# Seven of eleven gate/up chunks by seven products, with weight sums made by accumulating loads

## The chip, the cores and the metric

One core of one Trainium2 chip runs the whole layer as one program. Engines: PE (TensorE, matmuls into PSUM), PEld (its weight loads), DVE (VectorE), ACT (ScalarE), POOL (GpSimd), SP (issues DMAs). The metric is the device time of one execution in microseconds; the median of three runs of the kernel before is 2265.83 us (2264.74 to 2266.03).

## The reference

A layer of 256 tokens, width 2048, float32: a feed-forward, a mixer (mLSTM and stick-breaking attention), a second feed-forward, each followed by a layer norm, then a gated embedding. What the change touches is the feed-forward, of width 5632, run twice:

```
h = silu(x @ w1) * (x @ w3)        # gate and up, 2048 -> 5632
y = h @ w2                         # down, 5632 -> 2048
x = layer_norm(alpha * x + 0.5 * y)
```

## The kernel before

**Precision and weights.** Every product is made of three matmuls: activations and weights are split into a high and a low part (fp32r), and high·high, high·low and low·high are summed in PSUM (lines 990 to 992). A weight tile is 256 rows by 512 columns, 512 KB. It goes through `loads` (SP issues the DMA into a `raw` tile), then `split_one`: ACT casts the high half (L943), DVE subtracts for the low half (L945). `limits` says how many raw tiles and how many split weights may be held at once: in the feed-forwards 8 raws and 7 splits. One split weight takes two of the 44 pages of 4 KB per partition, a raw one.

**Units.** A `Unit` is one weight tile against one half of the tokens (128 rows): 2 row blocks x 3 matmuls = 6 matmuls of 128x512. `program` is the list of all units in the order in which PE runs them; side work (evictions, transposes) is scheduled between them by due times in `DELAY`. After each unit `splits_due` issues splits ahead, as far as `limits` allows, and each freed raw lets `loads` issue the next DMA. PE, DVE, ACT, POOL and SP each run their own instructions in that order.

**Direct chunks.** The width 5632 is cut into 11 chunks of 512 columns. `up(c)` does a chunk directly: 16 weight tiles (8 of w1, 8 of w3), each used by both token halves, 32 units. Gate results get SiLU on ACT, then DVE multiplies them with the up results (L388) and `turn` transposes the hidden tile on PE (L234); ACT and DVE split the transposed tile (L228, L229) into `hT`. `down(c, m)` multiplies m chunks of hidden by w2: 16 units per chunk, 8 weight tiles per chunk, and one DVE addition into `xres` per 512 columns, token half and call (L435).

**Seven-product chunks.** `up7(c)` does a chunk by a scheme of seven block products in place of eight (Winograd's form of Strassen's). The two token halves are the rows, the two halves of a 512-row group of the inner dimension the middle, and w1 and w3 the two column blocks. It takes 28 units with 28 weights: 8 raw weights for products 1 and 2, and for each of four row groups i five: products 5, 7, 6, 4, 3. The weights of the last five are b11, b12 (w1 and w3, first half of the group), b21, b22 (second half) and their sums, made by DVE in place (L295) by `minus`:

```
T1 = b12 - b11   (product 5)      T3 = b22 - b12   (product 7)
T2 = b22 - T1    (product 6)      T4 = b21 - T2    (product 4)      b22 (product 3)
```

Each row group takes four loads and four such subtractions. The matching sums of the activations ("forms") are made once per 512 columns by `form_turn` (L254). At the end of a product `done` combines the results in PSUM on DVE (L397).

**Order.** `weave(main, side)` spreads the units of one seven-product chunk evenly through a list of direct units. Before, each feed-forward has five woven stretches, one for each of chunks 1, 3, 5, 7 and 9; the other six chunks are direct. In the middle of it a stretch is gate(c), down of two earlier chunks, up(c), 64 units, with the 28 of the seven-product chunk between.

Of the kernel before, what the change touches and what calls it, by code (L numbers as in the profile page):

```python
# [11 lines left out]
ALU = mybir.AluOpType  # L12
# [14 lines left out]
TEMP_BUFS = 6  # L27


RAW_FFN, RAW_MIX, RAW_EDGE = 8, 5, 4  # L30
SPLIT_FFN, SPLIT_MIX, SPLIT_EDGE = 7, 6, 11
EDGE = 6
PSUM_BUFS = 8
SKEW = 6
# [12 lines left out]
class Sched:  # L47


    def __init__(self):  # L50
        self.now = 0.0
        self.heap = []
        self.count = 0
# [46 lines left out]
class Raw:  # L100


    def __init__(self, src, cols):
        self.src, self.cols, self.tile = src, cols, None


class Weight:
# [38 lines left out]
def flat(pairs):  # L146
    return [u for p in pairs for u in p]


def skewed(pairs):  # L150
    return [p[0] for p in pairs] + [p[1] for p in pairs]
# [3 lines left out]
def kernel(  # L155
# [6 lines left out]
    nc = tc.nc  # L162
    x, out = x[0], out[0]
# [56 lines left out]
    def load_x(c, t):  # L220
        cs = slice(c * COL, (c + 1) * COL)
        nc.sync.dma_start(out=xres[t][:, cs], in_=x[t * P:(t + 1) * P, cs])
# [22 lines left out]
    def form_turn(act, c):  # L245

        a = [act.whole[c][:, t * COL:(t + 1) * COL] for t in range(TT)]
        s12, s34 = temp(), temp()
        l, r = slice(0, 2 * P), slice(2 * P, 4 * P)
        for dst, in0, in1, op in ((s12[:, l], a[1][:, l], a[1][:, r], ALU.add),  # L250
                                  (s12[:, r], s12[:, l], a[0][:, l], ALU.subtract),
                                  (s34[:, l], a[0][:, l], a[1][:, l], ALU.subtract),
                                  (s34[:, r], a[0][:, r], s12[:, r], ALU.subtract)):
            nc.vector.tensor_tensor(out=dst, in0=in0, in1=in1, op=op)  # L254
        for h, src in enumerate((s12, s34)):
            dst = act.forms.get(c, h)
            split_psum(dst[:, 0], dst[:, 1], src.rearrange("q (k s) -> q k s", s=P))
            drop()
            act.forms.mark(c, h, 4)
        return  # L260
        yield
# [19 lines left out]
    def seven(wa, wb, rows, col0, cols, act, done):  # L281

        n = rows // (4 * P)
        accs = {m: {} for m in range(1, 8)}

        def unit(m, i, tile, src, half, sub):  # L290
            return Unit(tile, half, accs[m], src, i, sub, i == 0, i == n - 1, lambda ps, t, m=m: done(m, ps))

        def minus(out, a, b):
            def make():
                nc.vector.tensor_tensor(out=out.tile[:, :, :cols], in0=a.tile[:, :, :cols], in1=b.tile[:, :, :cols],  # L295
                                        op=ALU.subtract)
            return make

        units = []
        for m, sub in ((1, 0), (2, 2)):  # L300
            for i in range(n):
                units.append(unit(m, i, plain(rows_of(wa, (4 * i + sub) * P, col0, cols)), act, 0, sub))
        for i in range(n):
            b11, b12, b22, b21 = (rows_of(w, (4 * i + sub) * P, col0, cols)
                                  for w, sub in ((wa, 0), (wb, 0), (wb, 2), (wa, 2)))
            units += [
                unit(5, i, Weight(b11, [b11, b12], [], minus(b11, b12, b11)), act.forms, 0, 0),
                unit(7, i, Weight(b12, [b22], [b12], minus(b12, b22, b12)), act.forms, 1, 0),
                unit(6, i, Weight(b11, [], [], minus(b11, b22, b11)), act.forms, 0, 2),
                unit(4, i, Weight(b21, [b21], [b11, b21], minus(b21, b11, b21)), act, 1, 2),  # L310
                unit(3, i, Weight(b22, [], [b22]), act.forms, 1, 2),
            ]
        return units

    program = []
# [54 lines left out]
    def ffn(w1, w3, w2, act, norm, skew=True):  # L370
        n = FF // COL
        hT = ActT(act_tile)

        def turn(src, c, t):
            transposed(src, hT, c, t)
            drop()
            return
            yield

        def up(c):  # L380
            s = {}

            def gate(ps, t):
                s[t] = temp()
                activate(s[t][:], ps, ACT.Silu)

            def hidden(ps, t):
                nc.vector.tensor_tensor(out=s[t][:], in0=ps, in1=s[t][:], op=ALU.mult)  # L388
                sched.spawn(turn(s[t], c, t), DELAY["h"] + 2.0 * t)

            return group(w1, 0, D, c * COL, COL, act, gate), group(w3, 0, D, c * COL, COL, act, hidden)

        def up7(c):
            r, held = {}, {}

            def both(out, a, b, op):
                nc.vector.tensor_tensor(out=out, in0=a, in1=b, op=op)  # L397

            def done(m, ps):
                held[m] = ps  # L400
                if m == 1:
                    r["u"] = temp()
                    nc.scalar.copy(r["u"][:], ps)
                elif m == 2:
                    r["g0"] = temp()
                    both(r["g0"][:], ps, r["u"][:], ALU.add)
                    activate(r["g0"][:], r["g0"][:], ACT.Silu)
                elif m == 6:
                    u, v, z = r["u"], temp(), temp()
                    both(u[:], ps, u[:], ALU.add)  # L410
                    both(v[:], held[5], u[:], ALU.add)
                    both(u[:], held[7], u[:], ALU.add)
                    both(z[:], held[5], u[:], ALU.add)
                    r["v"], r["z"] = v, z
                elif m == 4:
                    u, z = r["u"], r["z"]
                    both(u[:], u[:], ps, ALU.subtract)
                    activate(u[:], u[:], ACT.Silu)
                elif m == 3:
                    u, v, z = r["u"], r["v"], r["z"]  # L420
                    both(v[:], ps, v[:], ALU.add)
                    both(v[:], v[:], r["g0"][:], ALU.mult)
                    both(z[:], z[:], u[:], ALU.mult)
                    drop(2)
                    sched.spawn(turn(v, c, 0), DELAY["h"])
                    sched.spawn(turn(z, c, 1), DELAY["h"] + 2.0)

            return seven(w1, w3, D, c * COL, COL, act, done)

        def down(c, m):  # L430
            pairs = []
            for g in range(D // COL):
                def add(ps, t, g=g):
                    xs = xres[t][:, g * COL:(g + 1) * COL]
                    nc.vector.scalar_tensor_tensor(out=xs, in0=ps, scalar=0.5, in1=xs,  # L435
                                                   op0=ALU.mult, op1=ALU.add)
                    if c + m == n:
                        norm.chunk(t, g)
                pairs += group(w2, c * COL, m * COL, g * COL, COL, hT, add, c)
            return pairs  # L440

        gate, hidden = up(0)
        program.extend((skewed(gate[:SKEW]) if skew else flat(gate[:SKEW])) + flat(gate[SKEW:]))
        gate2, hidden2 = up(2)
        program.extend(weave(flat(hidden + gate2 + down(0, 1) + hidden2), up7(1)))
        for c in range(4, n - 1, 2):
            gate, hidden = up(c)
            program.extend(weave(flat(gate + down(c - 3, 2) + hidden), up7(c - 1)))
        gate, hidden = up(n - 1)
        mid = down(n - 4, 2)  # L450
        program.extend(weave(flat(gate + hidden + mid[:12]), up7(n - 2)))
        program.append(norm.load)
        program.extend(flat(mid[12:] + down(n - 2, 1)))
        tail = down(n - 1, 1)
        program.extend(flat(tail[:-SKEW]) + skewed(tail[-SKEW:]))
        boundary(True)
# [457 lines left out]
    def loads(most=len(raws)):  # L914
        while pos["load"] < most and pos["raw"] < limits(pos["split"])[0]:
            j = pos["load"]
            r = raws[j]
            r.tile = page_pool.tile([P, 2, COL], F32, name="raw", tag="page")
            for ks in pieces(j):
                nc.sync.dma_start(out=r.tile[:, ks, :r.cols], in_=r.src[:, ks])  # L920
                if j == 0 and ks.start == 0:
                    load_x(0, 1)
            pos["load"] += 1
            pos["raw"] += 1

# [24 lines left out]
        loads()  # L950

    def splits_due():
        most = pos["at"] + 3 if pos["at"] < 5 else len(weights)
        while pos["split"] < most and len(splits) < limits(pos["split"])[1]:
            split_one()

# [71 lines left out]
```

## Time and profile before

| | |
|---|---|
| Median of 3 runs | 2265.83 us |
| Profiled execution: time, span | 2265.87 us, 2264.1 us |
| Granted clock of PE, mean | 0.996 |
| Busy: PE, DVE, ACT, POOL | 2235.6, 1652.4, 1137.3, 45.6 us |
| Bytes moved, mean rate | 476.65 MB, 211 GB/s |
| Queue of SP's DMAs, share of the 16 engines' span | 66.9% |
| Weight splits on DVE (L945) | 941, 1106.9 us |
| Weight sums on DVE (L295) | 160, 195.0 us |

How to read it: busy time is a sum over stages that differ, so the stages are looked at one by one. In a line of a group the numbers after the bar are its busy time, the mean of one in ns, and the idle time of its engine just before it with what ended it. A line of waits has who waited for whom: total us, times, longest. A line of a stretch has, for each engine, busy us and instructions, then the granted clock, the share of the DMA engines and GB/s.

### The profile page before, as it was taken

The numbers are of one execution on the slowest core, as the hardware profiler recorded it, in microseconds if no ns is written. First come the engines' busy times: TensorE is split into PE (matmuls) and PEld (weight loads), VectorE is DVE, ScalarE is ACT, GpSimd is POOL, SyncE is SP. The second block draws the span as 40 slices with busy tenths as digits, with TensorE's granted clock in tenths as the row PEclk, the third lists the DMA queues.
The fourth block names the chain that finished last, engine by engine and source line by source line (L and its number), as shares of the span: only waits on it lengthen the run. The fifth ranks groups of instructions, "written<-read, shape, count | busy, mean of one in ns | idle before, by whom it ended". The sixth has DMA issues, their size and how long they took to land.

```text
span 2264.1 us, 27326 instructions
## 1 busy us (share of the span) xinstructions
PE 2235.6 (99%) x10203; PEld 1851.5 (82%) x10203; DVE 1652.4 (73%) x1806; ACT 1137.3 (50%) x1327; POOL 45.6 (2%) x47
## 2 busy tenths in 40 slices
PE   8999999999999999999999999999999999999999
PEld 6888888888887888888888888778888888888878
DVE  5888878788888765654445466698787878887873
ACT  6545555555552555544643354355545545464452
POOL 2000000000000000100100000200000000000000
PEclk9999999999999999999999999999999999999999
DMA  8676767767783665565566676567677777777543
GB/s 303 217 240 217 248 209 247 234 215 242 251 277 110 206 187 160 169 185 158 167 183 189 186 227 213 174 205 243 204 243 229 223 241 233 241 237 260 196 152 100
DMA packets 249798, 476.65 MB, mean 211 GB/s; under 512 B 14976, under 2 KB 24000, under 8 KB 249664
## 3 DMA queue, kind: packets, MB, share of 16 engines
q1 hardware_dynamic: 249664, 474.90, 66.9%
q8 instruction: 80, 1.31, 0.2%
q14 instruction: 54, 0.44, 0.1%
HBM read 472.74 MB, written 2.10 MB: 210 GB/s over the span
## 4 chain that ended last, share of the span: by engine, by line
PE 93%; DVE 4%; DMA 1%; ACT 1%; issue 1%; SPq 0%; ACTq 0%; DVEq 0%
PE mm L992 30%; PE mm L990 30%; PE mm L991 30%; DMA raw<-in_ffn_w_dram 1%; PE ms L234 1%; DVE split L945 1%; DVE xres L352 1%; DVE xres L353 0%; ACT split L943 0%; DVE xres L350 0%; DVE actT L229 0%; DVE stats L337 0%; PE ms L715 0%; PE ms L738 0%; PE ms L666 0%
## 5 line engine op out<-in xcount | busy, mean ns | idle before, releaser
L945 DVE TENSOR_TENSOR split<-raw,split 128x1024 fp32r<-128x1024 f32 (+1 forms) x941 | 1106.9, 1203 | 343.0 <-ACT split L943 332.2
L990 PE MATMUL mm<-split,actT 128*128 128x512 f32 (+2 forms) x3200 | 1246.8, 390 | 4.8 <-ACT actT L228 4.8
L992 PE MATMUL mm<-split,actT 128*128 128x512 f32 (+2 forms) x3200 | 1236.9, 387 | 10.1 <-DVE actT L229 10.1
L991 PE MATMUL mm<-split,actT 128*128 128x512 f32 (+2 forms) x3200 | 1235.2, 386 | 0.7 <-DVE split L945 0.6
L943 ACT CAST split<-raw 128x1024 fp32r<-128x1024 f32 (+1 forms) x941 | 937.8, 1036 | 500.6 <-DVE raw L295 185.3
L992 PEld LDWEIGHTS mm<-split,actT 128*128 128x128 f32 x3200 | 602.8, 188 | 135.3 <-DVE actT L229 13.8
L990 PEld LDWEIGHTS mm<-split,actT 128*128 128x128 f32 x3200 | 603.3, 189 | 123.6 <-ACT actT L228 6.3
L991 PEld LDWEIGHTS mm<-split,actT 128*128 128x128 f32 x3200 | 603.3, 189 | 119.4 <-DVE split L945 1.9
L295 DVE TENSOR_TENSOR raw<-raw 128x1024 f32<-128x1024 f32 x160 | 195.0, 1219 | 0.0
L228 ACT CAST actT<-ms 128x512 fp32r<-128x512 f32 (+2 forms) x110 | 55.6, 522 | 133.2 <-PE ms L234 104.8
L435 DVE SCALAR_TENSOR_TENSOR xres<-mm,xres 128x512 f32<-128x512 f32 x112 | 76.9, 689 | 49.6 <-PE mm L992 49.4
L229 DVE TENSOR_TENSOR actT<-ms,actT 128x512 fp32r<-128x512 f32 (+2 forms) x110 | 64.2, 603 | 32.0 <-ACT actT L228 32.0
L206 ACT ACTIVATE temp<-temp 128x512 f32<-128x512 f32 (+1 forms) x36 | 21.0, 585 | 115.9 <-DVE temp L397 93.7
L397 DVE TENSOR_TENSOR temp<-mm,temp 128x512 f32<-128x512 f32 x60 | 41.4, 690 | 36.5 <-PE mm L992 35.5
L206 ACT ACTIVATE temp<-mm 128x512 f32<-128x512 f32 (+1 forms) x34 | 19.2, 572 | 64.5 <-PE mm L992 64.4
L206 ACT ACTIVATE big<-mm 128x512 f32<-128x512 f32 x20 | 12.0, 598 | 55.8 <-PE mm L992 55.8
L786 DVE TENSOR_TENSOR big<-mm,big 128x512 f32<-128x512 f32 x16 | 11.1, 692 | 30.0 <-PE mm L992 30.0
L872 DVE TENSOR_TENSOR temp<-temp,big 128x512 f32<-128x512 f32 (+1 forms) x10 | 5.8, 584 | 37.0 <-ACT temp L206 37.0
L367 POOL TENSOR_SCALAR xres<-xres 128x512 f32<-128x512 f32 x16 | 25.7, 1607 | 333.4 <-DVE xres L350 300.5
L202 ACT ACT_TABLE_LOAD x25 | 32.1, 1283 | 0.4
L206 ACT ACTIVATE rstd<-mv,eps 128x1 f32<-128x1 f32 x6 | 1.8, 295 | 53.9 <-DVE mv L343 53.9
L614 DVE SCALAR_TENSOR_TENSOR temp<-ms,cw,temp 128x253 f32<-128x253 f32 (+2 forms) x48 | 23.1, 481 | 7.4 <-ACT temp L206 6.2
(109 smaller groups left out, 473.7 us busy)
## 6 DMA issues: line engine op xcount, KB each, us to landing
raw<-in_ffn_w_dram SPq DMA_DIRECT2D x607, 512.0 KB, 4.7
raw<-in_w_in_dram SPq DMA_DIRECT2D x168, 512.0 KB, 3.8
raw<-in_w_out_dram SPq DMA_DIRECT2D x32, 512.0 KB, 5.0
raw<-in_w_ple_gate_dram SPq DMA_DIRECT2D x24, 512.0 KB, 4.7
raw<-in_w_up_m_dram SPq DMA_DIRECT2D x16, 512.0 KB, 3.7
raw<-in_w_up_sb_dram SPq DMA_DIRECT2D x16, 512.0 KB, 4.8
raw<-in_w_ple_gate_dram SPq DMA_DIRECT2D x16, 256.0 KB, 5.0
big<-in_ln_g_dram SPq DMA_DIRECT2D x6, 512.0 KB, 6.6
```

The costliest lines, as they stand in the source:

```text
L202: nc.scalar.preload_act_table_set(table[0])
L206: nc.scalar.activation(out, in_, func, **kw)
L228: nc.scalar.copy(hi, ps)
L229: nc.vector.tensor_tensor(out=lo, in0=ps, in1=hi, op=ALU.subtract)
L295: nc.vector.tensor_tensor(out=out.tile[:, :, :cols], in0=a.tile[:, :, :cols], in1=b.tile[:, :, :cols], op=ALU.subtract)
L397: nc.vector.tensor_tensor(out=out, in0=a, in1=b, op=op)
L435: nc.vector.scalar_tensor_tensor(out=xs, in0=ps, scalar=0.5, in1=xs, op0=ALU.mult, op1=ALU.add)
L943: nc.scalar.copy(hi[:, ks], r[:, ks])
L945: nc.vector.tensor_tensor(out=lo[:, ks], in0=r[:, ks], in1=hi[:, ks], op=ALU.subtract)
L990: nc.tensor.matmul(ps, hi, w[0][:, k, :u.cols], start=first, stop=False)
L991: nc.tensor.matmul(ps, hi, w[1][:, k, :u.cols], start=False, stop=False)
L992: nc.tensor.matmul(ps, lo, w[0][:, k, :u.cols], start=False, stop=last)
```

## The change

Seven chunks of each feed-forward (1, 2, 4, 5, 7, 8, 10) are done by seven products, four (0, 3, 6, 9) directly. All seven are woven as one list of 196 units into one list of 248 direct units; gate 0 and eight units of up 0 go ahead, and the rest of the down product follows.

The weight sums change sign: T1 = b12 + b11, T3 = b12 + b22, T2 = T1 + b22, T4 = b21 + T2, and the forms and the PSUM work take the signs up (`scalar=-1.0` in two places). T1 is no longer made by DVE: b12 is loaded by SP into the tile, and POOL issues a second load of b11 that adds into it (`accum_op`). T3 is made so for odd i, from a load of its own of b12; for even i it is a load of b12 to which DVE adds b22. T2 and T4 stay DVE's. In the feed-forwards nine raws and six split weights are held, and the limit of the first splits (`splits_due`) holds until weight 7 instead of 5.

```diff
-RAW_FFN, RAW_MIX, RAW_EDGE = 8, 5, 4
-SPLIT_FFN, SPLIT_MIX, SPLIT_EDGE = 7, 6, 11
+RAW_FFN, RAW_MIX, RAW_EDGE = 9, 5, 4
+SPLIT_FFN, SPLIT_MIX, SPLIT_EDGE = 6, 6, 11
...
-        for dst, in0, in1, op in ((s12[:, l], a[1][:, l], a[1][:, r], ALU.add),
-                                  (s12[:, r], s12[:, l], a[0][:, l], ALU.subtract),
-                                  (s34[:, l], a[0][:, l], a[1][:, l], ALU.subtract),
-                                  (s34[:, r], a[0][:, r], s12[:, r], ALU.subtract)):
-            nc.vector.tensor_tensor(out=dst, in0=in0, in1=in1, op=op)
+        nc.vector.tensor_tensor(out=s12[:, l], in0=a[1][:, r], in1=a[1][:, l], op=ALU.subtract)
+        nc.vector.scalar_tensor_tensor(out=s12[:, r], in0=s12[:, l], scalar=-1.0, in1=a[0][:, l],
+                                       op0=ALU.mult, op1=ALU.subtract)
+        nc.vector.tensor_tensor(out=s34[:, l], in0=a[0][:, l], in1=a[1][:, l], op=ALU.subtract)
+        nc.vector.tensor_tensor(out=s34[:, r], in0=a[0][:, r], in1=s12[:, r], op=ALU.add)
...
-        def minus(out, a, b):
+        def plus(out, a, b):
             def make():
                 nc.vector.tensor_tensor(out=out.tile[:, :, :cols], in0=a.tile[:, :, :cols], in1=b.tile[:, :, :cols],
-                                        op=ALU.subtract)
+                                        op=ALU.add)
...
+            t1 = Raw(b12.src, cols, b11.src)
+            t3, add = (Raw(b12.src, cols, b22.src), None) if i % 2 else (b12, plus(b12, b12, b22))
             units += [
-                unit(5, i, Weight(b11, [b11, b12], [], minus(b11, b12, b11)), act.forms, 0, 0),
-                unit(7, i, Weight(b12, [b22], [b12], minus(b12, b22, b12)), act.forms, 1, 0),
-                unit(6, i, Weight(b11, [], [], minus(b11, b22, b11)), act.forms, 0, 2),
-                unit(4, i, Weight(b21, [b21], [b11, b21], minus(b21, b11, b21)), act, 1, 2),
+                unit(5, i, Weight(t1, [t1], []), act.forms, 0, 0),
+                unit(7, i, Weight(t3, [t3, b22], [t3], add), act.forms, 1, 0),
+                unit(6, i, Weight(t1, [], [], plus(t1, t1, b22)), act.forms, 0, 2),
+                unit(4, i, Weight(b21, [b21], [t1, b21], plus(b21, t1, b21)), act, 1, 2),
                 unit(3, i, Weight(b22, [], [b22]), act.forms, 1, 2),
             ]
...
-        gate, hidden = up(0)
-        program.extend((skewed(gate[:SKEW]) if skew else flat(gate[:SKEW])) + flat(gate[SKEW:]))
-        gate2, hidden2 = up(2)
-        program.extend(weave(flat(hidden + gate2 + down(0, 1) + hidden2), up7(1)))
-        for c in range(4, n - 1, 2):
-            gate, hidden = up(c)
-            program.extend(weave(flat(gate + down(c - 3, 2) + hidden), up7(c - 1)))
-        gate, hidden = up(n - 1)
-        mid = down(n - 4, 2)
-        program.extend(weave(flat(gate + hidden + mid[:12]), up7(n - 2)))
+        gate, hidden = zip(*(up(c) for c in (0, 3, 6, 9)))
+        program.extend((skewed(gate[0][:SKEW]) if skew else flat(gate[0][:SKEW])) + flat(gate[0][SKEW:]))
+        last = down(8, 2)
+        main = flat(hidden[0] + down(0, 1) + gate[1] + down(1, 1) + hidden[1] + down(2, 2)
+                    + gate[2] + down(4, 1) + hidden[2] + down(5, 2)
+                    + gate[3] + down(7, 1) + hidden[3] + last[:8])
+        program.extend(main[:8] + weave(main[8:], [u for c in (1, 2, 4, 5, 7, 8, 10) for u in up7(c)]))
         program.append(norm.load)
-        program.extend(flat(mid[12:] + down(n - 2, 1)))
+        program.extend(flat(last[8:]))
...
+            if r.plus is not None:
+                nc.gpsimd.dma_start(out=r.tile[:, :, :r.cols], in_=r.plus, accum_op=ALU.add)
...
-        most = pos["at"] + 3 if pos["at"] < 5 else len(weights)
+        most = pos["at"] + 3 if pos["at"] < 7 else len(weights)
```

In `done` of `up7` the same instructions stand with other signs: product 4 is added instead of subtracted, product 3 subtracted instead of added, and the last multiplication of z is a `scalar_tensor_tensor` with the factor -1.

More of the change, by code (lines that the diff above doesn't have):

```diff
@@ L100, with __init__ @@
 class Raw:
-    def __init__(self, src, cols):
-        self.src, self.cols, self.tile = src, cols, None
+    def __init__(self, src, cols, plus=None):
+        self.src, self.cols, self.plus, self.tile = src, cols, plus, None
 class Weight:
@@ L415, in done @@
                 elif m == 4:
-                    u, z = r["u"], r["z"]
-                    both(u[:], u[:], ps, ALU.subtract)
+                    u = r["u"]
+                    both(u[:], ps, u[:], ALU.add)
                     activate(u[:], u[:], ACT.Silu)
@@ L420, in done @@
                     u, v, z = r["u"], r["v"], r["z"]
-                    both(v[:], ps, v[:], ALU.add)
+                    both(v[:], ps, v[:], ALU.subtract)
                     both(v[:], v[:], r["g0"][:], ALU.mult)
-                    both(z[:], z[:], u[:], ALU.mult)
+                    nc.vector.scalar_tensor_tensor(out=z[:], in0=z[:], scalar=-1.0, in1=u[:],
+                                                   op0=ALU.mult, op1=ALU.mult)
                     drop(2)
```

## The prediction

> **What bounds the kernel now.** I read the page's first two parts, then busy time by stretches, then the waits of PE, the groups, the DMA queue and one timeline.
>
> ```profile
> span 2264.1 us, 27326 instructions
> PE 2235.6 (99%) x10203; PEld 1851.5 (82%) x10203; DVE 1652.4 (73%) x1806; ACT 1137.3 (50%) x1327; POOL 45.6 (2%) x47
> ...
> PE 93%; DVE 4%; DMA 1%; ACT 1%; issue 1%; SPq 0%; ACTq 0%; DVEq 0%
> ```
>
> TensorE bounds it: 99% busy, 93% of the chain. So first count matmuls. The feed-forward stretches, where the change lies (columns: PE, PEld, DVE, ACT, POOL busy, granted clock, DMA share, GB/s):
>
> ```profile
> 0.00:40.00 40.00, 30.59 (x130) 23.23 (x131) 19.99 (x23) 22.62 (x31) 12.71 (x14) 0.96 0.98 352
> 160.00:280.00 120.00, 120.00 (x539) 99.44 (x538) 100.96 (x97) 63.09 (x66) 0.00 (x0) 1.00 0.73 231
> 280.00:400.00 120.00, 120.00 (x539) 99.44 (x538) 96.70 (x94) 61.07 (x64) 0.00 (x0) 1.00 0.72 229
> 70.00:150.00 80.00, 80.00 (x359) 66.22 (x358) 74.18 (x75) 43.20 (x47) 0.00 (x0) 1.00 0.71 223
> 1500.00:1510.00 10.00, 7.17 (x29) 5.58 (x28) 8.47 (x10) 4.61 (x6) 0.00 (x0) 0.83 0.48 152
> ```
>
> PE never idles at 160 to 400 us, DVE is 81 to 84% busy and DMA at 0.73. From 70 to 150 us DVE is 92.7% busy and PE still never idles. The saturated DMA rate is 352 GB/s (first row): 1.49 us for a 512 KB load.
>
> ```profile
> L945 DVE TENSOR_TENSOR split<-raw,split 128x1024 fp32r<-128x1024 f32 x60 | 72.5, 1221 | 15.6 <-ACT split L943 14.7
> L295 DVE TENSOR_TENSOR raw<-raw 128x1024 f32<-128x1024 f32 x16 | 19.5, 1219 | 0.0
> ```
> ```profile
> PE mm L992 <- DVE actT L229: 10.1, 7, 3.1
> PE mm L990 <- ACT actT L228: 4.8, 3, 4.0
> ```
> ```profile
> 1500.64 0.39 PE L992 MATMUL mm<-split,actT 128*128 128x512 f32 x1
> 1503.86 0.66 PE L234 MATMUL ms<-ident,temp 128*128 128x128 f32 x4 [2.83 <-DVE temp L388]
> ...
> 1506.23 0.63 PE L992 MATMUL mm<-split,actT 128*128 128x512 f32 x1
> 1506.65 0.63 PE L990 MATMUL mm<-split,actT 128*128 128x512 f32 x1
> ```
> ```profile
> raw<-in_ffn_w_dram SPq DMA_DIRECT2D x607, 512.0 KB, 4.7
> ```
>
> The first pair is one period of 127 us (174 to 301): 60 splits and 16 weight sums. The second shows that PE hardly waits for turned activations: 1.4 and 1.6 us a time. The timeline is one such wait: after 2.83 us idle the matmuls come every 0.42 us instead of 0.23, about eight of them, so 1.6 us more.
>
> **The change, part by part.**
>
> *Fewer units (removed).* A unit is 6 matmuls. Per feed-forward, a direct chunk has 32 units, a seven-product chunk 28, a chunk of the down product 16. Before 6x32 + 5x28 + 11x16 = 508, after 4x32 + 7x28 + 176 = 500. The chain shows the same event (8 transposes, 0.87 us) at 174.17, 301.15, 428.13, 555.11: 126.98 us for 92 units and 16 transposes of 0.109, so 1.361 us a unit. Two feed-forwards: 16 x 1.361 = **-21.8 us**, all on the path, since PE is full there. Transposes and chunks stay the same in number.
>
> *The woven stage.* 24 units go ahead of it and 32 follow it, so it holds 444: 604 us, with 80 transposes (9 us) 613 us in each feed-forward. Everything below is measured against 613.
>
> *DVE (moved and removed).* In the stage: 320 splits x 1.221 = 391, 10 weight sums per seven-product chunk (3, 2, 3, 2 by row group instead of 4 each) 70 x 1.219 = 85, and 143 PSUM additions, products and low halves x 0.69 = 99: 575 us, 94% of 613. The same sum for the old period gives 60 x 1.221 + 16 x 1.219 + 23 x 0.69 = 109 of 127, 86%, where the windows show 81 to 84%: successive instructions overlap (a split starts at 228.96, the next instruction at 230.10, the next at 231.24, 1.14 apart). So about 90% by the windows' measure. That is within the 92.7% held from 70 to 150 us with PE full. Cost nothing; cover: six splits held instead of seven, two in use, so four ahead at 613/320 = 1.92 us, 7.7 us. If it is gone, each microsecond that DVE is behind is a microsecond of PE.
>
> *Loads.* Plain ones per seven-product chunk stay 24; 6 accumulating ones come on POOL's queue (four for T1, two for T3). In the stage: 292 plain and 42 accumulating. Plain: 292 x 1.49 = 435 us of 613. No row shows an accumulating load. Let it occupy the DMA engines k times a plain one. k=1 (same bytes from HBM) is the low end; the high end by rows is 2.6, the longest landing of a weight load (11.8 us) over the median (4.6). I take 2: the tile comes in and the sum is read too. Use: k=1 498 us (81%), k=2 560 us (91%), k=2.6 598 us (98%). All fit, so no cost; from k=2.9 on DMA is the bound. [...]
>
> *Lateness of the summed tile.* The POOL load waits for the plain load into that tile to land, and behind it in POOL's queue stand only other such loads, and in the first feed-forward's head the scaling of x, done before. Nine raws, about 1.3 of them used but still held (T1 from product 5 to 4, b22 from 7 or 6 to 3), so 7.7 ahead at 613/292 = 2.1 us: 16 us from issue to cast. Two landings in a row need 4.7 + 4.7 = 9.4 us, at worst 4.7 + 11.8 = 16.5. Covered, the worst by the splits' 7.7 us. If the cover goes, ACT's cast waits, and behind it in order stand ACT's SiLUs and DVE's splits, then PE. SP's queue is not held: the sum is issued elsewhere. The ninth raw pays for two pages of the seventh split; pages in use do not grow.
>
> *Turns that come late (added).* Counting places in the woven list: chunk 0's hidden product ends with unit 37 and the down product of chunk 0 now starts at unit 39 (before: 23 units later). Chunk 2 ends at 149 and is used at 153 (before: 29). All other chunks have 8 or more between. Chunk 0's two halves are turned right at their use; chunk 2's first is, its second half covered: 3.5 tight turns per feed-forward. From the timeline at 301 us: transposes start 300.99, ACT's cast of the first four starts at 301.62 and takes 0.59, so 1.2 us to the high half, of which 0.44 is PE's own work; the low half, 0.68 more, is asked for 0.45 later. So 1.0 us if ACT and DVE are free; 3.3 us if each has just begun a weight (1.05 and 1.22). The waits shown average 1.4 and 1.6; I take 1.5, nearest to them: 7 x 1.5 = **+10.5 us** (7 to 23; at the far end the half clock of 1500 us adds 1.6 a time, up to 34). [...]
>
> *No cost:* signs in the forms and in the PSUM work (same count, same 0.42 and 0.69 us rows), the start limit 5 to 7 (PE is fed by lookahead of three there in both), more `down` calls (64 additions for 56, counted above).
>
> **Sum.** The profiled execution is 2265.87 us (span 2264.1), 0.04 above the median 2265.83. 2265.9 - 21.8 + 10.5 = 2254.6, say **2255**.
>
> **Rivals.**
> - *The accumulating loads are too dear (slower).* For: no row prices them, and DMA has the least room (91%). Against: 352 GB/s was held at 0.98. It decides from k=2.9, where 435 + 62.6k passes 613 plus 5 us of stalls; the gain is gone 0.1 later. At k=3.3: 642 - 618 = 24 us twice, 2303; at k=4: 68 us twice, 2390. The same through lateness: beyond some 24 us from issue to use, each microsecond costs up to 42 per feed-forward. [...]
> - *DVE becomes the bound (slower).* If it can hold only the 84% of the busiest long stretch, 575/0.841 = 684, 66 us twice: 2387. If 92.7%, 620 us, 2 us twice: 2259. The second is likelier, since PE set the pace in the first. At 90%: 639, 21 twice: 2297.
> - *The turns are hidden:* ACT and DVE free, other units first: full gain, 2244.
> - *It comes to nothing:* turns at their far end (23 us): 2267.
>
> **Chances.** Forecast 0.47 (own range 2246 to 2261), hidden turns 0.12, nothing 0.07, loads 0.20, DVE 0.14. This kernel's runs spread by 0.06%, so 0.2% (4.5 us) tells a change. Faster 0.59, same 0.07, slower 0.34. The range 2243 to 2310 leaves out most of the loads' case (k over 3.3) and the far end of DVE's, about 0.17.
>
> **What would show it.** Right: some 96 fewer matmuls; PE 10.00 of 10 in the woven stage but for short waits on L228 or L229 near units 39 and 153; DVE about 90%; DMA share 0.85 to 0.95. Wrong: ACT's casts waiting for DMA, a DMA share at 0.98, or PE waiting for splits, or a landing of the accumulating loads over some 15 us.

## The result and the profile after

The changed kernel takes 2284.13 us (median of 4, 2283.69 to 2284.74) against 2265.81 us before: ratio 1.0082, 95% interval 1.0065 to 1.0099. It is 18.3 us slower; 2255 and faster was forecast.

The page of the changed kernel, first part and chain by engine:

```profile
span 2283.0 us, 27662 instructions
PE 2231.5 (98%) x10107; PEld 1840.8 (81%) x10107; DVE 1705.4 (75%) x1878; ACT 1177.3 (52%) x1379; POOL 146.6 (6%) x131
...
PE 89%; DVE 6%; DMA 2%; issue 2%; ACT 1%; SPq 0%; ACTq 0%; DVEq 0%
```

96 matmuls are gone (10203 to 10107), as counted, and PE is 4 us less busy, but the chain now runs 11% outside PE instead of 7%. Nothing replaced PE as the bound; PE waits more. Its waits in the changed kernel (total us, times, longest):

```profile
PE mm L995 <- DVE actT L229: 15.4, 13, 2.7
PE mm L993 <- ACT actT L228: 12.8, 9, 3.0
PE ms L234 <- DVE temp L400: 11.2, 10, 1.7
...
PE mm L993 <- ACT split L946: 1.6, 2, 1.1
...
PE mm L994 <- DVE split L948: 0.8, 1, 0.8
```

L228 and L229 make the high and low half of a turned tile, L400 the products in front of the transposes. Of the 28.2 us on L228 and L229, 9.1 lie outside the woven stages (at the start and between the feed-forwards). Waits on weights (L946, L948) are 2.4 us, all before 44 us, ahead of the first woven stage. So within the woven stages PE waits neither for loads nor for splits; it waits for the hidden tiles. Stretches of 20 us of the changed kernel, two with waits and a usual one:

```profile
80.00:100.00 20.00, 17.42 (x61) 13.44 (x60) 12.65 (x14) 9.20 (x10) 1.19 (x1) 0.78 0.56 152
240.00:260.00 20.00, 16.22 (x67) 12.69 (x66) 14.24 (x17) 8.77 (x13) 1.20 (x1) 0.83 0.61 175
280.00:300.00 20.00, 20.00 (x90) 16.57 (x89) 18.09 (x17) 11.22 (x11) 2.41 (x2) 1.00 0.95 290
```

The usual stretch looks as forecast: PE full, DVE 90%, DMA 0.95. In the others PE runs 61 and 67 matmuls instead of 90, and DVE and DMA are *less* busy: they are not what is short. The granted clock falls to 0.78 and 0.83. PE's timeline at the second, where chunk 2 ends and is used at once:

```profile
242.88 0.65 PE L234 MATMUL ms<-ident,temp 128*128 128x128 f32 x4 [0.50 <-DVE temp L400]
244.26 0.50 PE L993 MATMUL mm<-split,actT 128*128 128x512 f32 x1 [0.73 <-ACT actT L228]
244.59 0.40 PE L994 MATMUL mm<-split,actT 128*128 128x512 f32 x1
247.54 0.79 PE L995 MATMUL mm<-split,actT 128*128 128x512 f32 x1 [2.55 <-DVE actT L229]
248.13 0.63 PE L993 MATMUL mm<-split,actT 128*128 128x512 f32 x1
248.56 0.63 PE L994 MATMUL mm<-split,actT 128*128 128x512 f32 x1
```

PE stops three times for one tile: for the product ahead of the transposes, for the high half, for the low half. Then matmuls come 0.43 us apart instead of 0.23 until 252 us, at a granted clock of 0.50 (248 to 252 us). Why the low half takes 2.55 us is in DVE's order in the same stretch:

```profile
243.34 1.22 DVE L948 TENSOR_TENSOR split<-raw,split 128x1024 fp32r<-128x1024 f32 x1
244.47 0.68 DVE L391 TENSOR_TENSOR temp<-mm,temp 128x512 f32<-128x512 f32 x1
245.07 1.21 DVE L948 TENSOR_TENSOR split<-raw,split 128x1024 fp32r<-128x1024 f32 x1
246.21 0.68 DVE L391 TENSOR_TENSOR temp<-mm,temp 128x512 f32<-128x512 f32 x1
246.81 0.68 DVE L229 TENSOR_TENSOR actT<-ms,actT 128x512 fp32r<-128x512 f32 x1
```

ACT had the high half ready at 244.2, but DVE does four instructions first: two splits, and the two products of chunk 3, which ends beside chunk 2.

Added up (waits from PE's timeline; half clock as 20 us times one minus the granted clock of the stretch):

| us | first feed-forward | second |
|---|---|---|
| waits at chunk 0 | 6.0 | 6.6 |
| waits at chunk 2 | 3.8 | 3.8 |
| waits at four other ends of seven-product chunks | 5.1 | 5.1 |
| half clock behind chunk 0 and 2 | 8.6 | 7.0 |
| less the wait and half clock before at 1500 us (2.8 and 1.6) | | -4.4 |
| fewer units | -10.9 | -10.9 |
| sum | +12.6 | +7.2 |

Measured, by the last addition of each feed-forward on the chain (before 716.18 and 2143.40, after 727.52 and 2161.85): +11.3, and +7.1 more. The table comes within 1.3 us. It leaves out the start: at 50 us the changed kernel has done 176 matmuls and the kernel before 166, some 2.3 us in its favour, which would leave the first column 1.0 us short.

### The profile page after: what moved, and what is told of

It is laid out like the page before. It is cut to its first block, busy times and chain, and to the rows that moved or that the text cites. A ratio compares the mean times of both kernels' runs of the same rounds, so it can differ in the third digit from the quotient of the medians.

```text
span 2283.0 us, 27662 instructions
## 1 busy us (share of the span) xinstructions
PE 2231.5 (98%) x10107; PEld 1840.8 (81%) x10107; DVE 1705.4 (75%) x1878; ACT 1177.3 (52%) x1379; POOL 146.6 (6%) x131
## 3 DMA queue, kind: packets, MB, share of 16 engines
q1 hardware_dynamic: 258368, 491.68, 65.4%
q0 software_dynamic: 22848, 44.05, 11.3%
## 4 chain that ended last, share of the span: by engine, by line
PE 89%; DVE 6%; DMA 2%; issue 2%; ACT 1%; SPq 0%; ACTq 0%; DVEq 0%
PE mm L995 29%; PE mm L993 28%; PE mm L994 28%; DMA raw<-in_ffn_w_dram 2%; DVE split L948 1%; DVE temp L400 1%; PE ms L234 1%; ACT split L946 1%; DVE xres L355 1%; DVE xres L439 1%; DVE xres L356 0%; DVE actT L229 0%; DVE xres L353 0%; DMA xres<-in_x_dram 0%; DVE stats L340 0%
## 5 line engine op out<-in xcount | busy, mean ns | idle before, releaser
L948 DVE TENSOR_TENSOR split<-raw,split 128x1024 fp32r<-128x1024 f32 (+1 forms) x989 | 1155.0, 1202 | 308.7 <-ACT split L946 296.7
L995 PE MATMUL mm<-split,actT 128*128 128x512 f32 (+2 forms) x3168 | 1229.2, 388 | 15.4 <-DVE actT L229 15.4
L946 ACT CAST split<-raw 128x1024 fp32r<-128x1024 f32 (+1 forms) x989 | 976.6, 1035 | 429.1 <-DVE raw L296 193.0
L925 POOL DMA_DIRECT2D raw<-in_ffn_w_dram x84 | 101.2, 1205 | 1137.4 <-DMA raw<-in_ffn_w_dram 356.6
L296 DVE TENSOR_TENSOR raw<-raw 128x1024 f32<-128x1024 f32 x140 | 170.3, 1216 | 0.0
L228 ACT CAST actT<-ms 128x512 fp32r<-128x512 f32 (+2 forms) x110 | 56.4, 521 | 135.2 <-PE ms L234 109.7
L439 DVE SCALAR_TENSOR_TENSOR xres<-mm,xres 128x512 f32<-128x512 f32 x128 | 87.5, 686 | 42.3 <-PE mm L995 41.9
L229 DVE TENSOR_TENSOR actT<-ms,actT 128x512 fp32r<-128x512 f32 (+2 forms) x110 | 65.2, 602 | 40.5 <-ACT actT L228 40.5
L400 DVE TENSOR_TENSOR temp<-mm,temp 128x512 f32<-128x512 f32 x98 | 67.4, 688 | 33.3 <-PE mm L995 31.5
L234 PE MATMUL ms<-ident,temp 128*128 128x128 f32 x176 | 28.8, 292 | 11.2 <-DVE temp L400 11.2
L234 PEld LDWEIGHTS ms<-ident,temp 128*128 128x128 f32 x176 | 22.9, 150 | 20.1 <-DVE temp L400 15.4
```

What stands on the lines that cost most here:

```text
L228: nc.scalar.copy(hi, ps)
L229: nc.vector.tensor_tensor(out=lo, in0=ps, in1=hi, op=ALU.subtract)
L234: nc.tensor.transpose(ps[:, k], src[:, k * P:(k + 1) * P], ident[:])
L925: nc.gpsimd.dma_start(out=r.tile[:, :, :r.cols], in_=r.plus, accum_op=ALU.add)
L946: nc.scalar.copy(hi[:, ks], r[:, ks])
L948: nc.vector.tensor_tensor(out=lo[:, ks], in0=r[:, ks], in1=hi[:, ks], op=ALU.subtract)
```

## The experiments

Three theories. L: hidden tiles are turned and used too soon in PE's order, and the idle time costs half clock on top. D: the loads, above all the accumulating ones, are late. V: DVE is the bound.

**e1_down_later**: the down products come later in the direct list.

```diff
-        main = flat(hidden[0] + down(0, 1) + gate[1] + down(1, 1) + hidden[1] + down(2, 2)
-                    + gate[2] + down(4, 1) + hidden[2] + down(5, 2)
-                    + gate[3] + down(7, 1) + hidden[3] + last[:8])
+        main = flat(hidden[0] + gate[1] + down(0, 1) + hidden[1] + down(1, 1) + gate[2] + down(2, 2)
+                    + hidden[2] + down(4, 1) + gate[3] + down(5, 2)
+                    + hidden[3] + down(7, 1) + last[:8])
```

> The changed kernel with one edit: each down product of the direct list comes one gate or up product later, so that chunk 0's hidden tiles have 29 units between their end and their use instead of 1, and chunk 2's 32 instead of 3. Theory L (PE reaches the transposes and first uses of a hidden tile before it is ready): the PE waits on L228 and L229 at chunk 0 (6.0 and 6.6 us) and chunk 2 (3.8 each) go, and with them the half-clock stretches behind them (granted clock 0.78 to 0.91 in the 20 us windows there, some 12 us in all): 2284 - 20 - 12 = 2252; the waits of 0.9 to 1.7 us on L400 at the other ends of seven-product chunks stay. Theory D (the loads, above all the accumulating ones, are too slow) and theory V (DVE is the bound): the time stays within 5 us of 2284, since neither loads nor DVE work change.

Measured 2249.71 us, ratio to the kernel before 0.9931 (0.9916 to 0.9946): 34.4 us below the changed kernel, by an order alone. Theory L is borne out; D and V predicted no change. Left over in e1's waits are, as expected, those on L400; those on L229 all lie outside the woven stages:

```profile
PE ms L234 <- DVE temp L400: 13.3, 14, 1.7
PE mm L995 <- DVE actT L229: 6.9, 6, 2.7
```

**e2_turn_later**: in the changed kernel, only the turns of seven-product chunks later.

```diff
-                    sched.spawn(turn(v, c, 0), DELAY["h"])
-                    sched.spawn(turn(z, c, 1), DELAY["h"] + 2.0)
+                    sched.spawn(turn(v, c, 0), DELAY["h7"])          # h7 = 8.0, h stays 3.0
+                    sched.spawn(turn(z, c, 1), DELAY["h7"] + 2.0)
```

> The changed kernel with one edit: the transposes of the hidden tiles of a seven-product chunk are put into PE's order 8 and 10 us behind the end of the chunk instead of 3 and 5. Theory L: the ten waits of PE on L400 (11.2 us) go, the waits at chunk 0 and 2 stay: 2274. Theory V: DVE is behind for good, and the same idle time shows up a little later, at splits or at the later transposes: 2280 to 2284. Theory D: the same, 2280 to 2284, with ACT waiting for DMA.

Measured 2275.65 us, 1.0043 (1.0028 to 1.0058): 8.5 us below the changed kernel. The waits on L400 are gone and those at chunk 0 and 2 stay, so DVE was late by a fixed 1 to 2 us at chunk ends and not behind for good. Two waits of 2.8 us on L391, the product of chunk 3, are new. They stand at chunk 2, in place of its waits on L400 and of most of those on L229, so that chunk 2 costs some 4.5 us of waits in each feed-forward instead of 3.8; that is a part of why the gain is less than 10.

**e3_both**: both edits.

> Both edits together. Theory L: both gains, 2284 - 32 - 10 = 2242, some 24 us faster than the kernel before, PE without waits in the woven stage. Theories D and V: no faster than 2275; PE waits for splits or ACT for DMA.

Measured 2235.15 us, 0.9863 (0.9847 to 0.9880): 30.5 us faster than the kernel before. A stretch of e3:

```profile
500.00:620.00 120.00, 120.00 (x541) 99.43 (x540) 108.79 (x109) 68.77 (x74) 10.84 (x9) 1.00 0.97 293
```

PE is full with DVE at 91% and DMA at 0.97. It is 49.0 us below the changed kernel, 7 more than expected; the table's waits and half clock in the changed kernel add up to 46.0 of them.

**e4_no_accum**: e3 without accumulating loads.

```diff
-            t1 = Raw(b12.src, cols, b11.src)
-            t3, add = (Raw(b12.src, cols, b22.src), None) if i % 2 else (b12, plus(b12, b12, b22))
+            t1, t3, add = b11, b12, plus(b12, b12, b22)
             units += [
-                unit(5, i, Weight(t1, [t1], []), act.forms, 0, 0),
-                unit(7, i, Weight(t3, [t3, b22], [t3], add), act.forms, 1, 0),
+                unit(5, i, Weight(t1, [b11, b12], [], plus(b11, b12, b11)), act.forms, 0, 0),
+                unit(7, i, Weight(t3, [b22], [t3], add), act.forms, 1, 0),
```

> Both edits, and T1 and T3 made by DVE from the four plain loads (16 weight sums per seven-product chunk instead of 10, no accumulating load). Theory V and my sum: DVE gets 42 x 1.22 = 51 us more in a woven stage of 613 us, 626 us by the sum of durations, about 98% with the overlap of instructions: PE waits come back, 10 to 60 us slower than with both edits, 2252 to 2300. Theory D: the DMA engines are relieved by 84 loads of 3.1 us, and the time falls below that of both edits.

Measured 2235.59 us, 0.9867 (0.9853 to 0.9882): the same as e3. Neither expectation held. D falls: taking the loads away gains nothing. But V falls too, and with it my own sum: DVE is 96% busy and PE does not wait. The same stretch of e4:

```profile
500.00:620.00 120.00, 120.00 (x541) 99.50 (x540) 115.08 (x115) 65.59 (x72) 0.00 (x0) 1.00 0.79 253
```

So with seven chunks the accumulating loads were not needed at all. The change of signs, which e4 keeps, is there for their sake.

**e6_no_accum_old_order**: the same edit as e4 on the changed kernel in its own order.

> The changed kernel in its own order, with T1 and T3 made by DVE from plain loads. Theory L: the waits at chunk 0 and 2 are the latency of the turns and stay; DVE is fuller (96% in e4), so its additions at the chunk ends come no earlier: 2280 to 2295. Rival D (the summed tiles come late, hold ACT and DVE in order, and so make the turns late): the waits shrink, 2250 to 2272.

Measured 2285.41 us, 1.0085 (1.0070 to 1.0100), 1.3 us above the changed kernel, within what the two intervals allow. PE's waits are the same kind (15.4 us on L228, 14.8 on L229, 12.6 on the products). The slowdown has nothing to do with how the sums are made.

**e9_before_down_early**: the kernel before, with only chunk 0's down product moved up.

```diff
-        program.extend(weave(flat(hidden + gate2 + down(0, 1) + hidden2), up7(1)))
+        program.extend(weave(flat(hidden + down(0, 1) + gate2 + hidden2), up7(1)))
```

> The kernel before with one edit: down of chunk 0 stands right behind hidden 0 (as in the changed kernel), gate 2 behind it; loads, sums, split limits and the five chunks are as before. Theory L (a hidden tile used too soon costs PE its latency and then half clock): in each feed-forward PE waits 4 to 6 us on L228 and L229 at chunk 0 and runs some 3 to 7 us' worth slower behind it: 2266 + 14 to 26 = 2280 to 2292. Rival (the place costs only where DMA or DVE are as full as in the changed kernel): 2266 to 2270.

Measured 2289.27 us, 1.0103 (1.0088 to 1.0118): 23.5 us slower, by one swapped pair of names in a kernel whose chunks, loads and limits are those of before. PE's waits in the first feed-forward of e9:

```profile
76.68 0.65 PE L234 MATMUL ms<-ident,temp 128*128 128x128 f32 x4 [0.85 <-DVE temp L388]
80.28 0.80 PE L990 MATMUL mm<-split,actT 128*128 128x512 f32 x1 [2.94 <-ACT actT L228]
83.05 0.80 PE L992 MATMUL mm<-split,actT 128*128 128x512 f32 x1 [1.54 <-DVE actT L229]
90.35 0.65 PE L990 MATMUL mm<-split,actT 128*128 128x512 f32 x1 [2.43 <-ACT actT L228]
91.73 0.80 PE L992 MATMUL mm<-split,actT 128*128 128x512 f32 x1 [0.30 <-DVE actT L229]
```

8.1 us of waits, 80 to 100 us at a granted clock of 0.74 (5.2 us); in the second feed-forward 9.4 us and 1510 to 1530 us at 0.68 (6.4 us). Less the 4.4 us that the kernel before had there: 24.7, against 23.5 measured.

**e5_before_h8**: the kernel before with all turns later (`"h": 3.0` to `8.0`).

> The kernel before with one edit: all turns of hidden tiles 8 us (and 10) behind their end instead of 3 (and 5). Theory L: the one wait of 2.8 us on L388 in the second feed-forward and the half clock behind it go: 2261. Then the rest of what the reordered kernel gains over the kernel before (30.5 us) comes from its fewer units. Rival: a good part of that gain came from later turns in general, 2250 or less.

Measured 2261.01 us, 0.9981 (0.9971 to 0.9990): 4.8 us, as expected. So of e3's 30.5 us, by the count of units 21.8 are units, and some 4.8 later turns. Of the 3.9 left the traces point to the start, though no run took it apart: at 50 us e3 has done 177 matmuls and the kernel before 166 (11 x 0.227 = 2.5 us).

**e7_all_t3_accum**: e3 with T3 by accumulating loads in all four row groups.

```diff
-            t3, add = (Raw(b12.src, cols, b22.src), None) if i % 2 else (b12, plus(b12, b12, b22))
+            t3, add = Raw(b12.src, cols, b22.src), None
```

> e3 with T3 made by an accumulating load in all four row groups (56 instead of 42 per feed-forward, 8 sums on DVE per chunk instead of 10). The changed kernel's trace has an accumulating load at 3.07 us of the 16 engines (11.3% of 2283 us over 84) and a plain one at 1.59, and a DMA share of 0.90 to 0.97 in the woven stage. If the share is a true measure of what is left, 14 x 3.07 = 43 us more do not fit into 613: DMA becomes the bound, PE waits for splits, 2235 + 10 to 50 = 2245 to 2285. If the share overstates it, 2235.

Measured 2235.36 us, 0.9869 (0.9854 to 0.9883): no loss beyond 0.5 us of waits on L391, with the DMA engines at a share of 1.00:

```profile
500.00:620.00 120.00, 119.49 (x535) 98.72 (x534) 104.94 (x105) 67.55 (x73) 15.64 (x13) 1.00 1.00 302
```

So the second expectation held: the share overstates how full they are (the changed kernel even shows 1.05 from 20 to 40 us). A plain load's landing went from 6.1 us (e3) to 7.1, so queueing is probably counted in; that was not shown. Where DMA would become the bound was not found.

**e8_eight, e8b_eight_t1, e10_eight_no_accum**: eight chunks by seven products (0, 4, 8 direct), with T1 and half of T3, with T1 alone, and with nothing by accumulating loads.

```diff
+        gate, hidden = zip(*(up(c) for c in (0, 4, 8)))
...
+        main = flat(hidden[0] + gate[1] + down(0, 1) + hidden[1] + down(1, 1) + down(2, 1) + gate[2] + down(3, 2)
+                    + down(5, 1) + hidden[2] + down(6, 1) + down(7, 2))
+        program.extend(main[:8] + weave(main[8:], [u for c in (1, 2, 3, 5, 6, 7, 9, 10) for u in up7(c)]))
...
+        program.extend(flat(down(9, 1)))
```

> e3 with eight of eleven chunks by seven products (chunks 0, 4, 8 direct), the down products again well behind their chunks. 8 units fewer in all: 2235.2 - 8 x 1.361 = 2224. DVE by the sum of durations 606 us in a woven stage of 608 (e4 had 626 in 613 and lost nothing), DMA 300 x 1.59 + 48 x 3.07 = 624 us of engine time in 608 (e7 had 636 in 613 and lost nothing): no new bound. If either is at its end here, PE waits for splits and the time is 2230 to 2260.

> e8 with T3 made by DVE in all row groups, so that only T1 comes by accumulating loads. DVE 625 us by durations in 608 (103%), DMA 575 (95%): 2224 as e8, or up to 2235 if DVE's end lies just above e4's 102%.

> e8 without accumulating loads: 16 sums on DVE per chunk, 665 us by durations in 608 (109%); by e4's ratio of busy time to durations (96% for 102%) 103% of the stage. DVE becomes the bound: PE waits for splits, 2224 + 2 x 20 = 2264 (2240 to 2290). Rival: DVE still keeps up and accumulating loads are worth nothing here either, 2224.

Measured 2241.98 us, 0.9898 (0.9881 to 0.9916); 2251.34 us, 0.9934 (0.9919 to 0.9950); 2322.13 us, 1.0248 (1.0231 to 1.0264). All three came out slower than forecast: 18 us over the 2224 of e8, 16 us over the 2235 that e8b was given at most, 32 us over the 2290 that e10 was given at most. Here the accumulating loads pay, 80 us between e10 and e8, and DVE's work is what e10 has more of. A stretch of e10 has DVE at 95% with PE no longer full:

```profile
380.00:500.00 120.00, 115.14 (x502) 91.68 (x501) 113.98 (x114) 65.43 (x71) 0.00 (x0) 1.00 0.73 242
```
DMA is at 0.73 there and ACT at 55%, so DVE is the bound. Its busy share does not tell by itself: e4 had 96%, with 541 matmuls in 120 us instead of 502. PE's waits in e10 have splits in the first place, 40 times:

```profile
PE mm L991 <- DVE split L945: 26.6, 40, 1.2
PE ms L234 <- DVE temp L390: 17.7, 7, 5.0
```

e8 itself did not gain the 11 us of its units: 8.7 us of waits on L391, the product of a direct chunk whose turn comes 3 us behind it.

**e11_eight_h8**: e8 with `h` at 8.0 too.

> e8 with the turns of the direct chunks also 8 and 10 us behind their end. In e8 PE waits 8.7 us (4 times) on L391, the multiplication that a direct chunk's turn needs, once 4.3 us in the second feed-forward with half clock behind it (some 1.6 us); with these gone 2242 - 10 = 2232, below e3's 2235. If DVE's lag at 94 to 96% busy only shows up elsewhere (PE on splits, 3.2 us in e8), 2237 to 2242, and eight chunks are no better than seven.

Measured 2231.28 us, 0.9846 (0.9829 to 0.9862), the fastest of all, 35 us below the kernel before, as expected; waits on L391 are gone. It lies 3.9 us below e3 where its units would give 10.9. PE waits 4.6 us on splits in it, against 2.4 in e3, so DVE's end may be near; where the other 5 us lie was not taken apart.

## Why the prediction was wrong

- *Fewer units, -21.8 us*: right. 96 matmuls are gone, and with the waits removed the gain is there (e3).
- *DVE at no cost*: right, and too cautious. About 90% was forecast; 90% was measured in the usual stretch above, and 89% in e3 from 100 to 620 us. I set the end by the 92.7% I had seen; in e4's woven stage PE had next to no waits with DVE at 96%, 102% by the sum of durations. e8b, at 103%, lost 9 us against e8 (99.7%), and e10, at 109%, 80 us. e10 took 98 us more than its units would give, 49 a stage, so that 665 us of work took some 657, 101%. From e4, e8b and e10 I estimate the end at about 101 to 103% of summed durations.
- *Loads at no cost*: right. The page after has the software queue at 11.3% of 2283 us for 84 loads, 3.07 us each, and a plain load at 65.4% over 938, 1.59 us: k = 1.93. I had taken 2, an argument between the rows' ends of 1 and 2.6.

```profile
q1 hardware_dynamic: 258368, 491.68, 65.4%
q0 software_dynamic: 22848, 44.05, 11.3%
...
raw<-in_ffn_w_dram SPq DMA_DIRECT2D x639, 512.0 KB, 5.8
...
raw<-in_ffn_w_dram POOLq DMA_DIRECT2D x84, 512.0 KB, 8.6
```

  The 1.93 is from packet times; whether they count queueing was not shown. Nor was it shown that the sum is read too, which was my reason for 2. The point k=2.9 from which DMA was to decide is a use of 613 us; e7's loads take some 615 by its own measured times (292 x 1.54 + 56 x 2.97), come up to it and cost nothing; no run went clearly past it. Nor is 352 GB/s the top rate: the kernel before shows 383 GB/s from 20 to 40 us. The sign "a DMA share at 0.98" for being wrong was no good either: the changed kernel has 1.02 from 200 to 220 us with PE full.
- *Lateness of the summed tile at no cost*: right. 5.8 + 8.6 = 14.4 us median for the two landings, under the 16 us ahead (the longest landing of an accumulating load was 12.1); e6 shows that taking them away changes nothing.
- *Turns that come late, +10.5 us*: this step failed. It named the mechanism and both places, but priced them by the mean of the waits of before (1.5 us), and none of those ten waits lies in a woven stage. All are at the start or between the feed-forwards, the longest of them here:

```profile
36.38 0.51 PE L990 MATMUL mm<-split,actT 128*128 128x512 f32 x1 [4.01 <-ACT actT L228]
728.72 0.50 PE L992 MATMUL mm<-split,actT 128*128 128x512 f32 x1 [2.72 <-DVE actT L229]
1448.13 0.50 PE L992 MATMUL mm<-split,actT 128*128 128x512 f32 x1 [3.11 <-DVE actT L229]
```

  So they say nothing of a hidden tile that is used at once. Nor does the count come out: two halves of chunk 0 and one of chunk 2 are 3 tight turns per feed-forward, not 3.5, and 6 x 1.5 is 9. Measured at these six: 20.2 us of waits, 3.4 a turn, beside the 3.3 that I had worked out for engines just begun on a weight; and 15.6 us of half clock; less 4.4 that had been there, 31.4. That is near the far end that I worked out (34) and set aside. Two things were mis-sized. One tile makes PE stop two times at chunk 0 and three times at chunk 2, not once, and at chunk 2 DVE's order puts four instructions ahead of the low half. And the half clock is not a rare extra: it followed at every one of the four places (granted clock 0.78 and 0.83 in the stretches shown, 0.83 from 1500 to 1520 us and 0.91 from 1680 to 1700).
- *"All other chunks have 8 or more between"*: wrong as a test. PE does not stop at the first use but at the transposes, which the due time puts 3 us behind the chunk's end; at the end of a seven-product chunk DVE has three instructions (2.1 us) and the splits in front of them, and missed it by 0.9 to 1.7 us at four ends in each feed-forward: 10.2 us in all, a term that the sum had at nothing. The row at 1503 us (2.83 us on L388) showed just this before.
- Of the rivals, the slower ones that I priced (loads, DVE) were the wrong ones, together 0.34; the right mechanism stood among them only as "it comes to nothing", at 0.07, because I let its far end stop at the 23 us without the clock. Even with the 34, the sum would have been 2278: the 10.2 us at the other chunk ends are in none of the rivals. The DVE rival was also priced in two measures: 575 us by durations, divided by shares (84%, 92.7%) that count overlap once.

## What to carry to other kernels

When an order written out by hand is changed, list for every produced tile what stands between its last input and the first instruction of the *bounding* engine that needs it, transposes included, and price a tight place as the whole chain through the in-order queues of all engines, plus the slow clock that can follow it (15.6 us here). PE at 99% hid nothing: two names swapped in a list cost 23.5 us here, more than the 21.8 us of the 16 units saved. Before work is taken off a second engine at some cost elsewhere, try whether that engine is short at all: at 96% DVE was not with seven chunks.

## What the runs showed of the hardware

- The clock of PE halved behind idle time that was never longer than 2.55 us in one piece: in the changed kernel 0.50, 0.73 and 2.55 us within 6 us at 242 to 248 us, then 0.43 us a matmul for some 4 us, at a granted clock of 0.50 from 248 to 252 us.
- The length of the waits does not settle by itself whether the clock halves. Single waits of 0.87 to 1.69 us at the other chunk ends of the changed kernel left it at 1.00, and so did the 3.11 us at 1448 us in the kernel before (1.00 from 1448 to 1454 us, 0.23 us a matmul). Two waits of 1.15 and 0.76 us near 42 us in the changed kernel were followed by 0.43 us a matmul and a granted clock of 0.56 from 44 to 46 us. What decides was not found.
- VectorE kept up at 96% busy, 102% by the sum of durations (e4, PE 120.00 of 120 us from 500 to 620): neighbouring instructions overlap by some 0.08 us (in the changed kernel those at 244.47, 245.07 and 246.21 us start before the one ahead has ended), so a sum a little over 100% still fits.
- A DMA share of 1.00 over 120 us, at 302 GB/s, cost nothing (e7, 2235.36 us against 2235.15 in e3).
